# The recurrence's three kinds of column sums share the accumulator banks of its scores, and the filler's matmuls rotate over three banks in place of two

## The chip, the cores and the metric

The kernel runs on one core of one Trainium2 chip. The metric is the device time of one execution in microseconds (us). The kernel before took 2701.37 us, the median of three runs that lay between 2699.15 and 2703.07 us. The names of the engines are those of the profile: PE multiplies matrices (PEld is its loading of the stationary matrix, which lies beside the multiplications), DVE is the vector engine, ACT the scalar engine, POOL the engine of small auxiliary work, SP the engine that issues most transfers (DMA).

## The reference, cut to what matters

The program is a decoder trunk of two layers over 1024 positions of width 1024, in float32. Each layer adds a mixer and then a gated feed-forward network (FFN) to the residual. The mixer of layer 0 is attention beside a pooling mixer; the mixer of layer 1 is a linear recurrence (RWKV-7) over 16 heads of 64 columns. The change touches the recurrence of layer 1 and the FFN work that runs beside it.

```python
kk = heads(k * k_k.astype(f32))
kk = kk / jnp.maximum(jnp.sqrt(jnp.sum(kk * kk, axis=-1, keepdims=True)), 1e-12)
...
def _rwkv7_step(state, inp):
    r_t, w_t, k_t, v_t, a_t, b_t = inp
    sa = jnp.einsum('bhvk,bhk->bhv', state, a_t)
    state = (state * w_t[:, :, None, :] + sa[..., None] * b_t[:, :, None, :]
             + v_t[..., None] * k_t[:, :, None, :])
    return state, jnp.einsum('bhvk,bhk->bhv', state, r_t)
...
mean = jnp.mean(y, axis=-1, keepdims=True)
var = jnp.mean(jnp.square(y - mean), axis=-1, keepdims=True)
y = ((y - mean) * lax.rsqrt(var + GN_EPS)).reshape(b, s, d) * ln_w.astype(f32) + ln_b.astype(f32)
bonus = jnp.sum(rh * kh * r_k.astype(f32), axis=-1, keepdims=True) * vh
...
def _swiglu(h, w_gate, w_up, w_down):
    return (jax.nn.silu(h @ w_gate) * (h @ w_up)) @ w_down
```

## The kernel before

Activations lie transposed: 128 channels on the partitions, 512 positions (one half of the sequence) along the free axis. So every large accumulator is 128x512 float32, which is one whole PSUM bank, and a core has eight banks. A large product is made in three matmuls, because each operand is split into a rounded high part and a low remainder: weight high by activation high (L163), weight high by activation low (L164), weight low by activation high (L165). For that each weight block is loaded by DMA into `wraw`, ACT casts it to `whi` (L151) and DVE makes `wlo` (L152). An output block of a projection takes 24 matmuls (8 blocks of the inner dimension by 3); a block of the FFN's down projection takes 12, since the 22 blocks of the FFN's hidden width are taken in groups of four.

**The recurrence.** One half of the sequence and eight heads make a job (`Rwkv.job`); there are four, in the order (heads 0 to 7, half 0), (heads 8 to 15, half 0), and later the same two for half 1. By the trace they begin at about 1050, 1284, 1776 and 2000 us. A job works in chunks of 64 positions and has three stages.

1. Preparation, for four pairs of heads one after the other. A pair loads decay, key, a, r and v, squares the key and sums the squares over each head's 64 channels by a matmul with a block matrix (L1025, result `ms`); ACT turns the sum into a reciprocal root (L1028, L1029) and DVE builds the operands `ZL` and `bk` with it (L1030, L1032, L1038, L1040). Then come the scores: four accumulators (two batches of chunks by two heads, L1056), which ACT and DVE evict into `XR` and `ZL` (L1061 to L1064). Small products with the identity and a centring matrix follow (L1070, L1081).
2. Inversion of the triangular blocks, on DVE: a transpose (L1092, L1095), 30 steps of two small operations (L1106, L1108), then the transposes back, into `t11` (L1116) and into `XR` (`back`, L1114). Two further rounds on PE finish it: `gps` (L1126) needs `t11`, its result is copied to `g` half by ACT (L121) and half by DVE (L123), and `xps` (L1136) needs both halves of `g`.
3. The serial loop over eight chunks (L1161, L1167, L1173, L1184, L1186), with the bonus of one pair beside every second chunk (`head_sum`, L970), then the group norm's sum of squares (L1201) and the four gated outputs (L1212, L1217 to L1219).

**The filler.** The work beside a job is FFN work: in half 0 the second half's FFN of layer 0 (`f1`), in half 1 the output projection and the first half's FFN of layer 1 (`rest`). `weave` takes a step of the job and then as many filler matmuls as the numbers in `rw.fr` say. A filler block takes an accumulator from `k.mm`, here the tag `fm` of the pool `pf`. A gate block is read for the last time by DVE at L726, after three ACT operations (L723 to L725); an up block at L732; a down block by the residual add at L705.

**Banks and order.** A pool tile is asked for by tag and number of buffers, and the tags rotate: the n-th tile with the tag `s` of three buffers lies in the bank of the (n-3)-rd, and its first matmul waits until that one's last reader is done. During the jobs the eight banks were: tag `t` one (the three kinds of sums), tag `s` three (scores and the loop's first two products), tag `o` two, tag `fm` two. The order on each engine is fixed when the program is built, by a scheduler that reorders the recorded instructions; an engine runs its list strictly in order, so a matmul that waits for a bank holds back everything behind it on PE.

## Time and profile before

| what | value |
|---|---|
| median of the runs | 2701.37 us (2699.15 to 2703.07) |
| time of the profiled execution | 2699.03 us |
| its span from first to last instruction | 2697.2 us |
| PE busy | 2633.8 us (98%), 15368 matmuls |
| PEld busy | 2080.5 us (77%) |
| DVE busy | 1724.3 us (64%) |
| ACT busy | 1301.9 us (48%) |
| mean granted TensorE clock | 0.993 |

A busy time is the share in which an engine had an instruction under way; the rest is split by what ended the idle time. The chain of waits follows the work that ended last back from the last instruction. In rows of the trace the first two figures are the start and the duration in us; a bracket at the end gives the idle time of the engine just before the instruction, and who ended it. The granted clock of a stretch is 1.00 where PE runs at 2.4 GHz throughout; the other level is 1.2 GHz.

### The profile page before, as it was taken

The numbers are of one execution on the slowest core, as the hardware profiler recorded it, in microseconds if no ns is written. First come the engines' busy times: TensorE is split into PE (matmuls) and PEld (weight loads), VectorE is DVE, ScalarE is ACT, GpSimd is POOL, SyncE is SP. The second block draws the span as 40 slices with busy tenths as digits, with TensorE's granted clock in tenths as the row PEclk, the third lists the DMA queues.
The fourth block names the chain that finished last, engine by engine and source line by source line (L and its number), as shares of the span: only waits on it lengthen the run. The fifth ranks groups of instructions, "written<-read, shape, count | busy, mean of one in ns | idle before, by whom it ended". The sixth has DMA issues, their size and how long they took to land.

```text
span 2697.2 us, 40269 instructions
## 1 busy us (share of the span) xinstructions
PE 2633.8 (98%) x15368; PEld 2080.5 (77%) x15368; DVE 1724.3 (64%) x2940; ACT 1301.9 (48%) x2299; POOL 50.6 (2%) x139
## 2 busy tenths in 40 slices
PE   8999999999999999999999999999999999999999
PEld 6787878788888777777777677777777778888887
DVE  8777684654446655975995685469768856634443
ACT  7555564442224765534634466664445444332232
POOL 1000000000001000000000000000000000000000
PEclk9999999999999999999999999999999999999999
DMA  4111131233333546424523534454344336333333
GB/s 136 58 52 55 44 98 48 83 97 96 96 98 114 168 162 191 129 82 123 160 87 100 194 101 161 160 182 128 91 141 134 93 100 199 109 98 94 98 98 94
DMA packets 170817, 307.03 MB, mean 114 GB/s; under 512 B 18928, under 2 KB 25968, under 8 KB 170624
## 3 DMA queue, kind: packets, MB, share of 16 engines
q1 hardware_dynamic: 156800, 279.29, 33.6%
q10 hardware_dynamic: 13824, 25.17, 2.5%
q8 instruction: 120, 1.97, 0.3%
q14 instruction: 73, 0.60, 0.1%
HBM read 257.96 MB, written 46.43 MB: 113 GB/s over the span
## 4 chain that ended last, share of the span: by engine, by line
PE 77%; DVE 14%; DMA 3%; ACT 3%; issue 2%; SPq 0%; DVEq 0%; ACTq 0%
PE mm L163 16%; PE mm L164 16%; PE mm L165 16%; PE fm L163 6%; PE fm L164 5%; PE fm L165 5%; DVE wlo L152 2%; PE mm L175 1%; DVE nu L1108 1%; DVE pd L1106 1%; DMA wraw<-in_wu_dram 1%; DVE ZL L1064 1%; ACT whi L151 1%; PE o L1173 1%; PE s L1161 1%
## 5 line engine op out<-in xcount | busy, mean ns | idle before, releaser
L151 ACT CAST whi<-wraw 128x512 fp32r<-128x512 f32 x738 | 453.7, 617 | 867.4 <-PE mm L164 478.7
L152 DVE TENSOR_TENSOR wlo<-wraw,whi 128x512 fp32r<-128x512 f32 x738 | 501.3, 684 | 449.6 <-ACT whi L151 441.1
L163 PE MATMUL mm<-hh,whi 128*128 128x512 f32 x864 | 344.1, 400 | 6.2 <-ACT hh L355 6.1
L165 PE MATMUL mm<-hh,wlo 128*128 128x512 f32 x864 | 338.4, 392 | 0.0
L164 PE MATMUL mm<-hl,whi 128*128 128x512 f32 x864 | 337.9, 392 | 0.0
L163 PE MATMUL mm<-uh,whi 128*128 128x512 f32 x728 | 283.6, 391 | 0.9 <-DVE x L1317 0.9
L165 PE MATMUL mm<-uh,wlo 128*128 128x512 f32 x728 | 283.1, 390 | 1.0 <-DVE wlo L152 1.0
L164 PE MATMUL mm<-ul,whi 128*128 128x512 f32 x728 | 283.2, 390 | 0.0
L163 PE MATMUL fm<-h1h,whi 128*128 128x512 f32 x528 | 220.2, 417 | 14.8 <-DVE sg L726 9.9
L164 PE MATMUL fm<-h1l,whi 128*128 128x512 f32 x528 | 210.3, 398 | 0.1
L165 PE MATMUL fm<-h1h,wlo 128*128 128x512 f32 x528 | 209.5, 397 | 0.5 <-DVE wlo L152 0.5
L163 PEld LDWEIGHTS mm<-hh,whi 128*128 128x128 f32 x864 | 162.3, 188 | 43.4 <-ACT hh L355 7.8
L165 PEld LDWEIGHTS mm<-hh,wlo 128*128 128x128 f32 x864 | 162.5, 188 | 34.4 <-issue 0.2
L164 PEld LDWEIGHTS mm<-hl,whi 128*128 128x128 f32 x864 | 162.7, 188 | 33.1 <-DVE hl L260 1.7
L163 PE MATMUL fm<-hh,whi 128*128 128x512 f32 x416 | 170.9, 411 | 3.3 <-ACT hh L259 2.3
L164 PE MATMUL fm<-hl,whi 128*128 128x512 f32 x416 | 164.9, 396 | 0.2 <-DVE hl L260 0.2
L165 PE MATMUL fm<-hh,wlo 128*128 128x512 f32 x416 | 164.6, 396 | 0.0
L163 PEld LDWEIGHTS mm<-uh,whi 128*128 128x128 f32 x728 | 136.5, 188 | 34.6 <-issue 3.5
L164 PEld LDWEIGHTS mm<-ul,whi 128*128 128x128 f32 x728 | 136.6, 188 | 30.9 <-issue 1.1
L165 PEld LDWEIGHTS mm<-uh,wlo 128*128 128x128 f32 x728 | 136.7, 188 | 30.1 <-DVE wlo L152 1.8
L705 DVE TENSOR_TENSOR x<-mm,x 128x512 f32<-128x512 f32 x96 | 66.3, 692 | 119.3 <-PE mm L165 119.2
L163 PEld LDWEIGHTS fm<-h1h,whi 128*128 128x128 f32 x528 | 100.6, 191 | 47.1 <-DVE sg L726 12.2
(338 smaller groups left out, 4645.4 us busy)
## 6 DMA issues: line engine op xcount, KB each, us to landing
wraw<-in_wg_dram SPq DMA_DIRECT2D x176, 256.0 KB, 2.8
wraw<-in_wu_dram SPq DMA_DIRECT2D x176, 256.0 KB, 2.7
wraw<-in_wd_dram SPq DMA_DIRECT2D x176, 256.0 KB, 2.7
wraw<-in_w_in_dram SPq DMA_DIRECT2D x52, 256.0 KB, 2.9
x<-in_xT_dram SPq DMA_DIRECT2D x32, 256.0 KB, 4.6
x<-x SPq DMA_DIRECT2D x32, 256.0 KB, 3.3
wraw<-in_w_k_dram SPq DMA_DIRECT2D x32, 256.0 KB, 2.8
wraw<-in_w_v_dram SPq DMA_DIRECT2D x32, 256.0 KB, 3.0
```

What stands on the lines that cost most here:

```text
L151: k.nc.scalar.copy(hi[0:p, 0:n], raw[0:p, 0:n])
L152: k.nc.vector.tensor_tensor(lo[0:p, 0:n], raw[0:p, 0:n], rd(hi[0:p, 0:n]), ALU.subtract)
L163: nc.tensor.matmul(out, wh, xh, start=(first and i == 0), stop=False)
L164: nc.tensor.matmul(out, wh, xl, start=False, stop=False)
L165: nc.tensor.matmul(out, wl, xh, start=False, stop=(last and i == n - 1))
L175: k.nc.tensor.matmul(out[n * q:n * q + n], w[:, n * j:n * j + n], xs[j], start=c == 0, stop=c + g == len(xs), tile_position=(0, n * q))
L705: nc.vector.tensor_tensor(X[half][m], o, X[half][m], ALU.add)
L1064: nc.vector.tensor_tensor(ZL[h][HS[1 - h], i, bs], s4[HS[1]], self.msk[HS[1]].rearrange("p a t -> p (a t)").unsqueeze(1).broadcast_to([64, ...
L1106: nc.vector.tensor_tensor(pv, nu[:, j + 1:32, j:j + 1].broadcast_to([P, n, j]), nu[:, j:j + 1, 0:j].broadcast_to([P, n, j]), ALU.mult)
L1108: nc.vector.tensor_tensor(nu[:, j + 1:32, 0:j], nu[:, j + 1:32, 0:j], pv, ALU.add)
L1161: nc.tensor.matmul(z[HS[h], i], ZL[h][:, i, c, 0:64], SV[h][:, i, c], start=True, stop=True)
L1173: nc.tensor.matmul(sp[HS[h], i], BK[h][:, i, c], uv[h][:, i], start=True, stop=True)
```

## The change

Three accumulators of the recurrence no longer have a bank with the tag `t` of their own: the sum of squares of the key (L1022 asks for it, L1025 writes it), the bonus sum in `head_sum` (L968, L970) and the group norm's sum of squares (L1197, L1201). They ask for the tag `s` with `k.sbufs` buffers, which is three in both recurrence stages, and so take turns with the scores and with the loop's products. The bank that the tag `t` had goes to the filler: the tag `fm` gets three buffers in place of two, in the three places where the filler's accumulators are set. The count of banks stays at eight. Layer 0's attention keeps its tag `t`.

```diff
     def head_sum(self, src):
 
         k = self.k
-        o = pst(k, "t", 1)
+        o = pst(k, "s", k.sbufs)
...
             nc.scalar.activation(kn, kr, AF.Square, scale=cvec(k, "k_k", p))
-            ms = pst(k, "t", 1)
+            ms = pst(k, "s", k.sbufs)
...
         nc.scalar.copy(spread, raw)
-        z = pst(k, "t", 1)
+        z = pst(k, "s", k.sbufs)
...
-    f1 = using(k, f1, mm=(pf, "fm", 2), ntbufs=3)
+    f1 = using(k, f1, mm=(pf, "fm", 3), ntbufs=3)
...
-    k.mm, k.sigm, rw.ln_exp = (pf, "fm", 2), False, True
+    k.mm, k.sigm, rw.ln_exp = (pf, "fm", 3), False, True
...
-    project, rest = (using(k, g, mm=(pf, "fm", 2), ntbufs=3) for g in tail(0, tp, 4, False))
+    project, rest = (using(k, g, mm=(pf, "fm", 3), ntbufs=3) for g in tail(0, tp, 4, False))
```

No instruction is added or removed, but the scheduler sets some in another order.

**Place 1: PE, the first job, the sum `ms` of its second pair.** `t_9657` and `s_9657` are the same sum; `fm_9605` and `fm_9718` are filler blocks, `s_9495`, `s_9541` and `s_9542` scores of the first pair, `o_9620` its centred v. Before:

```order
L165 MATMUL fm_9605<-h1h_5371,wlo_9600 128x512
L1025 MATMUL t_9657<-kn_9655,cc 128x512
L163 MATMUL fm_9605<-h1h_5377,whi_9599 128x512
L164 MATMUL fm_9605<-h1l_5378,whi_9599 128x512
L165 MATMUL fm_9605<-h1h_5377,wlo_9600 128x512
L163 MATMUL fm_9718<-h1h_5335,whi_9706 128x512
L164 MATMUL fm_9718<-h1l_5336,whi_9706 128x512
L165 MATMUL fm_9718<-h1h_5335,wlo_9707 128x512
L1056 MATMUL s_9495<-ZL_2218_9414,bk_9483 128x128
```

Now:

```order
L164 MATMUL fm_9718<-h1l_5348,whi_9706 128x512
L1056 MATMUL s_9542<-ZL_2219_9415,bk_9483 128x128 x4
L1081 MATMUL o_9620<-cc,ld_9491 64x64 x16
L1025 MATMUL s_9657<-kn_9655,cc 128x512
L165 MATMUL fm_9718<-h1h_5347,wlo_9707 128x512
```

The sum stood ahead of the first pair's scores and now stands behind the last of them, 11 filler matmuls later; the second pair's scores come 17 filler matmuls later than they did. By the products at L1081 of the third pair the count of filler matmuls that stand ahead is the same as before. The fourth pair moves likewise (its sum by 30, its scores by 20 filler matmuls), and from its products at L1081 to the end of the job PE's list is the same. Over the four jobs, 6 of the 12 sums that follow another pair moved by 7 filler matmuls or more, the others by 0 or 1.

**Place 2: DVE, the end of the first job's inversion.** `sg_10570` belongs to the filler blocks `fm_10530` (gate) and `fm_10587` (up), `t_2457_10609` is `t11`, `g_10679` is DVE's half of `g`. Before:

```order
L1116 STREAM_TRANSPOSE t_2457_10609<-nu_10216 128x32x32
L1114 STREAM_TRANSPOSE XR_9416<-nu_10216 32x32x32 x2
L152 TENSOR_TENSOR wlo_10634<-wraw_10635,whi_10633 128x512
L152 TENSOR_TENSOR wlo_10741<-wraw_10742,whi_10740 128x512
L1114 STREAM_TRANSPOSE XR_9416<-nu_10216 32x32x32
L726 TENSOR_TENSOR sg_10570<-fm_10530,sg_10570 128x512
L1114 STREAM_TRANSPOSE XR_9416<-nu_10216 32x32x32
L152 TENSOR_TENSOR wlo_10797<-wraw_10798,whi_10796 128x512
L732 TENSOR_TENSOR sg_10570<-fm_10587,sg_10570 128x512
L152 TENSOR_TENSOR wlo_10817<-wraw_10818,whi_10816 128x512
L260 TENSOR_TENSOR h1l_10624<-sg_10570,h1h_10623 128x512
L123 COPY g_10679<-s_10646 32x512
```

Now:

```order
L1116 STREAM_TRANSPOSE t_2457_10609<-nu_10216 128x32x32
L1114 STREAM_TRANSPOSE XR_9416<-nu_10216 32x32x32 x2
L726 TENSOR_TENSOR sg_10570<-fm_10530,sg_10570 128x512
L152 TENSOR_TENSOR wlo_10741<-wraw_10742,whi_10740 128x512
L152 TENSOR_TENSOR wlo_10797<-wraw_10798,whi_10796 128x512
L1114 STREAM_TRANSPOSE XR_9416<-nu_10216 32x32x32
L732 TENSOR_TENSOR sg_10570<-fm_10587,sg_10570 128x512
L1114 STREAM_TRANSPOSE XR_9416<-nu_10216 32x32x32
L260 TENSOR_TENSOR h1l_10624<-sg_10570,h1h_10623 128x512
L123 COPY g_10679<-s_10646 32x512
L152 TENSOR_TENSOR wlo_10817<-wraw_10818,whi_10816 128x512
```

The last read of the gate block moved ahead of two weight remainders and a transpose; `wlo_10634` moved ahead of L1116 and `wlo_10817` behind the copy of `g`, so that one remainder less stands ahead of that copy.

**Place 3: DVE, the end of the second job.** `gn` are the four gated outputs, `x_4130` to `x_4467` the residual adds that free the down blocks `fm_14189`, `fm_14245`, `fm_14323` and `fm_14343`, in this order on PE. Before:

```order
L1218 SCALAR_TENSOR_TENSOR gn_14217<-gn_14217,cv,ld_14213 128x512
L1217 SCALAR_TENSOR_TENSOR gn_14232<-BK_2681_11850,cv,o_14226 128x512
L1219 TENSOR_TENSOR gn_14217<-gn_14217,ld_14215 128x512
L1218 SCALAR_TENSOR_TENSOR gn_14232<-gn_14232,cv,ld_14228 128x512
L705 TENSOR_TENSOR x_4130<-fm_14189,x_4130 128x512
L1219 TENSOR_TENSOR gn_14232<-gn_14232,ld_14230 128x512
L705 TENSOR_TENSOR x_4260<-fm_14245,x_4260 128x512
L152 TENSOR_TENSOR wlo_14378<-wraw_14379,whi_14377 128x512
L152 TENSOR_TENSOR wlo_14398<-wraw_14399,whi_14397 128x512
L705 TENSOR_TENSOR x_4367<-fm_14323,x_4367 128x512
L152 TENSOR_TENSOR wlo_14404<-wraw_14405,whi_14403 128x512
L705 TENSOR_TENSOR x_4467<-fm_14343,x_4467 128x512
```

Now:

```order
L1219 TENSOR_TENSOR gn_14202<-gn_14202,ld_14200 128x512
L1217 SCALAR_TENSOR_TENSOR gn_14217<-BK_2681_11850,cv,o_14211 128x512
L1217 SCALAR_TENSOR_TENSOR gn_14232<-BK_2681_11850,cv,o_14226 128x512
L1218 SCALAR_TENSOR_TENSOR gn_14217<-gn_14217,cv,ld_14213 128x512
L1218 SCALAR_TENSOR_TENSOR gn_14232<-gn_14232,cv,ld_14228 128x512
L1219 TENSOR_TENSOR gn_14217<-gn_14217,ld_14215 128x512
L1219 TENSOR_TENSOR gn_14232<-gn_14232,ld_14230 128x512
L705 TENSOR_TENSOR x_4130<-fm_14189,x_4130 128x512
L705 TENSOR_TENSOR x_4260<-fm_14245,x_4260 128x512
L705 TENSOR_TENSOR x_4367<-fm_14323,x_4367 128x512
L152 TENSOR_TENSOR wlo_14358<-wraw_14359,whi_14357 128x512
L152 TENSOR_TENSOR wlo_14378<-wraw_14379,whi_14377 128x512
```

All twelve operations on `gn` now stand ahead of the residual adds, and `wlo_14358`, which stood among them, stands behind the adds.

## Rows read from the trace of the kernel before

**Rows 1.** The page's busy times.

```profile
PE 2633.8 (98%) x15368; PEld 2080.5 (77%) x15368; DVE 1724.3 (64%) x2940; ACT 1301.9 (48%) x2299; POOL 50.6 (2%) x139
```

**Rows 2.** What PE waited for over the whole span: the waiting line, the releaser, the total in us, the number of waits, the longest.

```profile
PE fm L163 <- DVE sg L726: 13.2, 8, 4.0
...
PE fm L163 <- DVE x L705: 5.9, 6, 3.0
PE s L1056 <- DVE ZL L1064: 5.5, 6, 1.9
...
PE s L1126 <- DVE t L1116: 4.1, 2, 2.3
```

**Rows 3.** Busy time by stretch: start and end, length, then busy us (and instructions) of PE, PEld, DVE, ACT and POOL, the granted clock, the busy share of the DMA engines and GB/s. The stretches are preparation and inversion of the first job, the same of the second, and the inversion of the fourth up to PE's wait for `t11`.

```profile
1054.00:1118.00 64.00, 60.07 (x441) 45.94 (x441) 61.66 (x99) 37.73 (x71) 3.76 (x7) 0.97 0.48 150
1118.00:1161.50 43.50, 42.06 (x211) 33.88 (x210) 41.59 (x90) 21.14 (x38) 0.75 (x6) 1.00 0.34 104
...
1284.00:1352.00 68.00, 63.77 (x477) 48.63 (x478) 63.80 (x100) 40.98 (x74) 3.02 (x7) 0.97 0.48 145
1352.00:1391.00 39.00, 34.62 (x161) 27.95 (x158) 37.09 (x85) 17.33 (x31) 0.76 (x6) 0.97 0.35 102
...
2080.00:2125.00 45.00, 41.75 (x276) 33.41 (x276) 43.18 (x93) 19.94 (x35) 1.62 (x7) 1.00 0.29 89
```

**Rows 4.** The five longest of PE's waits for a filler bank, from its timeline.

```profile
1169.21 0.50 PE L163 MATMUL fm<-h1h,whi 128*128 128x512 f32 x1 [4.03 <-DVE sg L726]
...
1366.66 0.50 PE L163 MATMUL fm<-h1h,whi 128*128 128x512 f32 x1 [1.67 <-DVE sg L726]
1388.76 0.79 PE L163 MATMUL fm<-h1h,whi 128*128 128x512 f32 x1 [2.71 <-DVE sg L726]
...
1508.27 0.76 PE L163 MATMUL fm<-h1h,whi 128*128 128x512 f32 x1 [3.00 <-DVE x L705]
...
2050.06 0.50 PE L163 MATMUL fm<-gh,whi 128*128 128x512 f32 x1 [2.35 <-DVE sg L726]
```

**Rows 5.** Stretches around these five waits, columns as in rows 3.

```profile
1164.00:1178.00 14.00, 9.97 (x89) 7.50 (x88) 11.10 (x12) 3.05 (x5) 0.00 (x0) 0.76 0.28 78
1386.00:1396.00 10.00, 7.29 (x26) 5.88 (x26) 9.66 (x19) 2.35 (x5) 0.00 (x0) 0.83 0.22 62
1507.00:1513.00 6.00, 4.74 (x14) 3.84 (x15) 3.64 (x7) 0.35 (x1) 0.00 (x0) 0.72 0.55 177
2049.00:2055.00 6.00, 4.94 (x15) 3.90 (x16) 4.34 (x7) 3.88 (x7) 0.00 (x0) 0.72 0.39 122
...
1364.00:1372.00 8.00, 6.33 (x28) 4.91 (x27) 7.72 (x19) 3.53 (x6) 0.00 (x0) 1.00 0.38 108
```

**Rows 6.** The end of the first job's inversion: the timeline of DVE, and of PE from 1174 us on.

```profile
1173.92 0.70 DVE L123 COPY g<-s 32x512 f32<-32x512 f32 x1
...
1174.85 0.63 PE L164 MATMUL fm<-h1l,whi 128*128 128x512 f32 x1
...
1178.00 0.39 PE L164 MATMUL fm<-h1l,whi 128*128 128x512 f32 x1
...
1178.55 1.20 PE L1136 MATMUL s<-XR,g 32*32 32x32 f32 x64
```

**Rows 7.** The same place in the second job: DVE's copy of `g`, and PE.

```profile
1406.26 0.70 DVE L123 COPY g<-s 32x512 f32<-32x512 f32 x1
...
1407.31 1.20 PE L1136 MATMUL s<-XR,g 32*32 32x32 f32 x64
```

**Rows 8.** The end of the second job, from the timelines of DVE and of PE.

```profile
1498.94 0.69 DVE L705 TENSOR_TENSOR x<-fm,x 128x512 f32<-128x512 f32 x1
...
1507.43 0.69 DVE L705 TENSOR_TENSOR x<-fm,x 128x512 f32<-128x512 f32 x1
...
1504.87 0.40 PE L165 MATMUL fm<-h1h,wlo 128*128 128x512 f32 x1
```

**Rows 9.** The waits for `t11` in the third and fourth job, and the DVE operations that set when the fourth job's third batch of scores could start, with its start on PE.

```profile
1896.19 1.20 PE L1126 MATMUL s<-t,XR 32*32 32x32 f32 x64 [1.82 <-DVE t L1116]
...
2124.03 1.20 PE L1126 MATMUL s<-t,XR 32*32 32x32 f32 x64 [2.25 <-DVE t L1116]
...
2054.70 0.69 DVE L705 TENSOR_TENSOR x<-fm,x 128x512 f32<-128x512 f32 x1 [1.30 <-PE fm L165]
2055.31 0.68 DVE L1040 TENSOR_TENSOR bk<-ld,ld 128x512 f32<-128x512 f32 x1
...
2056.45 2.05 PE L1056 MATMUL s<-ZL,bk 64*128 64x128 f32 x24
```

**Rows 10.** The operations between a sum `ms` and the scores of its pair, of the first job, by line: count, busy us, mean ns of one, idle time before.

```profile
L1028 ACT ACTIVATE kn<-t,eps 128x512 f32<-128x512 f32 x6 | 4.1, 682 | 0.4 <-PE t L1025 0.4
L1029 ACT ACTIVATE kn<-kn 128x512 f32<-128x512 f32 x6 | 3.8, 630 | 0.1
...
L1032 DVE SCALAR_TENSOR_TENSOR ZL<-kn,cv,ep 64x512 f32<-64x512 f32 x11 | 8.2, 744 | 0.1
L1030 DVE SCALAR_TENSOR_TENSOR kn<-kn,ld 128x512 f32<-128x512 f32 x6 | 4.1, 685 | 0.0
L1038 DVE SCALAR_TENSOR_TENSOR ld<-kn,vc,ld 128x512 f32<-128x512 f32 x5 | 3.7, 750 | 0.1
L1040 DVE TENSOR_TENSOR bk<-ld,ld 128x512 f32<-128x512 f32 x5 | 3.4, 685 | 0.0
```

## The prediction

> **What bounds the kernel now.** I read the busy times first [rows 1]: PE is busy in 2633.8 of 2697.2 us, so all its idle time together is 63.4 us, and that is the most that any change of waits can give, but for the clock. The list of PE's waits comes next [rows 2]. The reader is to see that two of its entries are waits for a filler bank: L163 opens a filler block and can do so only when the block two before it has been read by L726 (13.2 us in 8 waits) or by L705 (5.9 us in 6), together 19.1 us. Their places [rows 4] are the inversions of the first two jobs, the end of the second job and the preparation of the fourth.
>
> Third comes the granted clock around these waits [rows 5]. After the wait of 4.03 us it averages 0.76 over 14 us, which is 14 x 0.24 = 3.4 us of full-speed work lost; after 2.71, 3.00 and 2.35 us it loses 10 x 0.17, 6 x 0.28 and 6 x 0.28, 1.7 us each time; around the wait of 1.67 us the clock stays at 1.00. A filler matmul's row reads 0.63 us in the slow stretch and 0.39 us behind it [rows 6]. So the four longest waits cost 8.5 us more than they show, and the whole account of the filler's banks is 19.1 + 8.5 = 27.6 us.
>
> Last I asked which engine was behind in these stretches [rows 3]. In preparation and inversion of the first job DVE was busy 61.66 of 64.00 and 41.59 of 43.50 us, idle 4.25 us in 107.5; in the second 63.80 of 68.00 and 37.09 of 39.00, idle 6.1 us in 107. PE idled 5.4 and 8.6 us in the same stretches, more than DVE. PE waited there because DVE was late with everything, the filler's reads among the rest. That decides most of the sum.
>
> **The change part by part.** No instruction comes or goes, so what counts is waits, order and clock.
>
> *The third bank, end of the second job.* PE stopped at 1505.27 us (1504.87 + 0.40) [rows 8] until L705 of `x_4130` had ended at 1508.1, and that add stood behind the output operations. With three banks the block that waited takes the bank of `fm_14150`, which L705 had freed at 1499.6. It runs from 1505.3 to about 1508.0 (12 matmuls by 0.23 us, from 28 in 6.33 us in the last of rows 5). The block behind it needs the bank of `fm_14189`. In the new order the twelve output operations stand ahead of that bank's add (place 3), but they are the same twelve that stood among what ran up to 1508, and one weight remainder less stands among them, so I expect the add near 1508 and no new wait. DVE is not saturated behind this place, and PE is the bound up to the norm. So the whole 3.00 us goes and the slow stretch with it: -4.7 us. The bounds are -4.7 and 0 (if the next block waits for its `wlo`, which now stands behind the adds).
>
> *The third bank, first job.* The waits there add up to 5.5 us (three of L726; the longest 4.03). But the step behind them, L1136, needs DVE's half of `g`. That copy ended at 1174.62 and L1136 began at 1178.55 [rows 6]; in the second job it began 0.35 us after the copy (1406.96 and 1407.31) [rows 7]. The slack is 3.93 - 0.35 = 3.6 us. One weight remainder less stands ahead of the copy (place 2), 0.6 to 0.7 us. So L1136 can come 4.2 us earlier, no more unless DVE idles less. The 4.03 us of idle time moves from L163 to L1126 and L1136, and a slow stretch follows it there, in work that PE alone bounds: 1.7 to 3.4 us given back. Net -0.8 to -2.5, and up to 2 us more if half of DVE's idle time goes. I take -2; bounds -5 and +1.
>
> *The third bank, second job.* The waits are 1.67 + 2.71 + 0.6 (two of L705) us, but L1136 began 0.35 us after the copy of `g`, so there is no slack at all. DVE could win back part of its 6.1 us; against that the slow stretch of 1.7 us that lay ahead of L1136, where PE had time, now lies behind it. I take 0; bounds -4 and +3.
>
> *The third bank, third and fourth job.* There L1126 itself waited 1.82 and 2.25 us for DVE's `t11` [rows 9]: a PE that comes sooner waits longer. In the fourth job the wait of 2.35 us at 2050 us is followed by scores that began at 2056.45, 0.5 us after DVE's last operand was ready (2055.31 + 0.68); DVE had idled 1.30 us there for the late filler block, and that goes. But PE then waits for the scores, with a slow stretch to follow. I take -0.5 for both jobs; bounds -4 and +2.
>
> *The sums in the ring of the scores.* This cost the trace of before doesn't show. `ms` of a pair must now wait until the third tile before it, the second of the four score tiles of the pair ahead, has been evicted, so it stands behind these scores (place 1). Behind `ms` come L1028, L1029, L1030, twice L1032, L1038 and L1040: 0.68 + 0.63 + 0.69 + 1.49 + 0.75 + 0.69 = 4.9 us until the pair's scores may start [rows 10]. Before, this ran beside the eviction of the pair ahead. It is hidden if DVE and PE have other work meanwhile. On PE they have: the scores of the first job's second pair come 17 filler matmuls, 17 x 0.23 = 3.9 us, later, and the lists agree again a pair later. On DVE the order puts `bk`, `ZL` and weight remainders of later steps there. From below it costs 0; from above the full 4.9 us for each pair but the first of the four jobs, 12 x 4.9 = 59 us, which is far out of reach, since only 6 of the 12 sums moved on PE by more than one filler matmul. I keep 0 and 8 us (half of 4.9 at three or four places) as ends and take +1, near the lower one, because the moved pair has work on both engines. The bonus sums and the norm's sum stand in the serial loop, where DVE has idle time and each tile is read before its bank comes round: 0, with the serial chain as the cover; if it were gone, one eviction of 0.7 us for each of 16 sums, 11 us.
>
> The sum is -4.7 - 2 + 0 - 0.5 + 1 = -6.2 us. Against the profiled execution's own 2699.03 us (span 2697.2, 1.8 us around it) that is 2692.8. The profiled execution was 2.3 us below the median of the runs, so for a median I add 2.3: 2695.1, rounded to 2695 us.
>
> The Trainium skill has a rule that would make more of it and one that would make less. "Perfetto Trace Analysis", section Identifying Performance Opportunities, says that gaps which repeat on the engine that should be saturated can mean too little PSUM for the next tile; the waits for filler banks are such gaps, and by that rule the whole account of rows 2 would go, the first rival below. The same page, Identifying the Most-Contended Engine, says to take occupancy for VectorE as a fair measure and to improve the busiest engine first; DVE's 96% in rows 3 bears that out for the inversions, and by it the banks give next to nothing there, the second rival.
>
> **The rivals.**
>
> - *The whole account goes.* All 19.1 us and the slow stretches' 8.5: 2701.4 - 27.6 = 2674; with half of it, 2688. For it: the waits are for banks, and the PE order is kept. Against it: DVE's idle time of 4.25 and 6.1 us.
> - *Given back.* PE's idle time only changes its name, from L163 to L1126, L1136 and L1056, also at the end of the second job, because of the `wlo` behind the adds. 2697 to 2703, the centre 2700. For it: rows 3 and 9. Against it: rows 8, where DVE had room soon after.
> - *Slower by the ring.* The sums bind the pairs of a job together: DVE idles while PE and ACT pass the 4.9 us from `ms` to the scores, so each inversion starts later, and since it ends in L1126 and L1136, for which PE already waits in two jobs, that delay is PE's. At 2 us for each of six moved sums it is +12, with the -4.7 of the end of job two +7: 2708. It decides from about 2 us of delay per moved sum. For it: DVE is the late engine in these stretches. Against it: the order gives DVE other operations meanwhile.
> - *The third bank is never reached*, because the scheduler put each block's read early anyway: then the waits at L163 stay, and the time is 2700. It can hardly be: in the built order the matmul that waited at 1508 us no longer waits for DVE.
>
> **How the numbers follow.** This kernel's measurement can tell about 0.2%, 5.4 us, from no change; so faster means below 2696. The forecast case, a gain of 3 to 12 us, has 0.49, of which 0.34 lies below 2696 and 0.15 above. The whole account or most of it (a gain over 12) has 0.16. Given back, with the bank never reached, has 0.21. Slower by the ring has 0.14. That makes faster 0.50, no change 0.36, slower 0.14. The likeliest case alone spans 2689 to 2699. The range of 8 in 10 goes from 2682 (some 70% of the whole account) to 2705 (the ring's lower prices).
>
> **What the profile would show.** The list of PE's waits has lost L163 for L726 and for L705 (under 3 us together). If I am right, L1126 and L1136 have gained several us for DVE, above all L1136 for the copy of `g` in the first two jobs; the wait at the end of the second job is gone, and the clock stays at 1.00 there; DVE's idle time in rows 3's stretches is about what it was. If the first rival is right, L1126 and L1136 wait no more than before and DVE idles less. If the ring costs, L1056 or L1025 wait longer, for L1064 or L1040, and DVE idles more ahead of L1030. I am wrong in size if PE's total idle time of 63.4 us falls by more than 15 us or grows, and wrong in the mechanism if the gain lies in the inversions of the first two jobs.

## The result and the profile after

The changed kernel takes 2711.36 us (median of 7 runs, 2705.91 to 2714.29) against 2699.96 us for the kernel before on the same chip (7 runs). The ratio is 1.0039, interval 1.0028 to 1.005, which is 10.5 us of 2700 (7.6 to 13.5). It is slower; the forecast was 2695 us, and the range ended at 2705. Medians below leave out two executions that took several times as long as the others, one of all_but_ms (6304.43 us) and one of early_ring_of_four (10087.19 us).

The profiled execution spans 2709.6 us. The page's busy times, which answer to [rows 1]:

```profile
PE 2634.0 (97%) x15368; PEld 2088.6 (77%) x15368; DVE 1725.0 (64%) x2940; ACT 1301.8 (48%) x2299; POOL 50.5 (2%) x139
```

PE does the same 2634 us of work. Its idle time went from 63.4 to 2709.6 - 2634.0 = 75.6 us, 12.2 of the 12.4 us between the spans. (That says where the time stands, not what caused it: the mean granted clock fell as well, from 0.993 to 0.988.) So the list of PE's waits is read next, with the columns of [rows 2]:

```profile
PE s L1056 <- DVE bk L1040: 15.0, 13, 3.8
PE s L1056 <- DVE ZL L1064: 8.8, 10, 1.7
PE s L1126 <- DVE t L1116: 7.5, 3, 3.7
...
PE s L1136 <- ACT g L121: 5.2, 1, 5.2
PE s L1136 <- DVE g L123: 3.4, 2, 2.1
...
PE mm L163 <- ACT hh L259: 2.9, 1, 2.9
...
PE fm L163 <- DVE x L705: 1.2, 2, 0.6
PE fm L163 <- DVE sg L726: 1.2, 1, 1.2
```

The reader is to see two things. The third bank did what it says: L163 waits 2.4 us for L705 and L726, where it waited 19.1 [rows 2]. But other entries have grown or are new: the scores (L1056) for `bk`, from 4.3 us in the listing by line of the kernel before to 15.0; the scores for L1064, the eviction of scores ahead, from 5.5 to 8.8; L1126 from 4.1 to 7.5; L1136, which is not in the list of the kernel before; and L163 of the layer's first product for `hh`, 2.9 us.

Where on the way is the time lost? A mark that comes once in each job is the first product of the serial loop, L1161. From the timeline of PE of the kernel before:

```profile
1193.49 0.69 PE L1161 MATMUL s<-SV,ZL 128*64 128x64 f32 x16
...
1422.25 0.69 PE L1161 MATMUL s<-SV,ZL 128*64 128x64 f32 x16
...
1917.49 0.69 PE L1161 MATMUL s<-SV,ZL 128*64 128x64 f32 x16
...
2146.37 0.69 PE L1161 MATMUL s<-SV,ZL 128*64 128x64 f32 x16
```

and of the changed kernel:

```profile
1195.08 0.69 PE L1161 MATMUL s<-SV,ZL 128*64 128x64 f32 x16
...
1427.83 0.69 PE L1161 MATMUL s<-SV,ZL 128*64 128x64 f32 x16
...
1927.06 0.69 PE L1161 MATMUL s<-SV,ZL 128*64 128x64 f32 x16
...
2154.02 0.69 PE L1161 MATMUL s<-SV,ZL 128*64 128x64 f32 x16
```

The delay is 1.6, 5.6, 9.6 and 7.7 us at the four marks, and 12.4 us at the end. So the second and third job lose 4 us each, the fourth wins 2 back, and nearly 5 us come behind the last job, in a place of which the prediction does not speak.

A mark comes from a single execution, and the runs show how much that leaves open. Four pairs of them run the same instructions in the same order on PE, DVE and ACT until 2290 us, since they differ only in where the last norm stands: the kernel before and norm_early_before, the changed kernel and tail_cover, and two pairs further below (the runs are told in the next section). Their marks differ by 0.2 to 1.7 us in 14 of 16 cases, and by 2.0 and 3.7 us in two. tail_cover has its marks at 1193.36, 1428.55, 1928.12 and 2154.20 us, so the large delays of the second and third job are there again, but the 1.6 us of the first job are not.

**The second job.** PE, ACT and DVE between the sum `ms` of its second pair and that pair's scores, from the timelines of the changed kernel (an idle time before an instruction and its releaser stand in brackets):

```profile
1298.03 1.02 PE L1025 MATMUL s<-kn,cc 128*128 128x512 f32 x2
...
1298.30 0.63 ACT L1008 ACTIVATE ep<-ld 128x512 f32<-128x512 f32 x1
1298.96 0.63 ACT L1016 ACTIVATE ld<-ld 128x512 f32<-128x512 f32 x1
1299.49 0.67 ACT L1028 ACTIVATE kn<-s,eps 128x512 f32<-128x512 f32 x1
...
1301.64 0.69 DVE L1030 SCALAR_TENSOR_TENSOR kn<-kn,ld 128x512 f32<-128x512 f32 x1
...
1305.12 0.68 DVE L705 TENSOR_TENSOR x<-fm,x 128x512 f32<-128x512 f32 x1
1305.72 0.68 DVE L1040 TENSOR_TENSOR bk<-ld,ld 128x512 f32<-128x512 f32 x1
...
1306.45 1.46 PE L1056 MATMUL s<-ZL,bk 64*128 64x128 f32 x16 [3.76 <-DVE bk L1040]
```

In the timeline of the kernel before, the second sum of this job ran at 1287.29 us, 16.8 us ahead of its scores:

```profile
1287.29 1.13 PE L1025 MATMUL t<-kn,cc 128*128 128x512 f32 x2 [0.35 <-ACT kn L1021]
...
1304.07 2.01 PE L1056 MATMUL s<-ZL,bk 64*128 64x128 f32 x22
```

Now it runs at 1298.03, behind all 32 scores of the pair ahead. From there the scores are not 4.9 but 8.4 us away: 1.0 us is the sum itself, which the 4.9 leave out, and on ACT the sum finds L1008 and L1016 ahead of it, on DVE other operations, an add of the filler (L705) among them. The filler on PE lasts until 1302.69, 4.7 us from the start of the sum, and then PE stands 3.76 us.

So the path was not made longer by the change; what went is the lead. In the kernel before, 7 of the 16 sums ran 12.5 to 18.7 us ahead of their pair's first scores, and the other 9 ran 7.4 to 9.3 us ahead. In the changed kernel all 16 run 7.2 to 9.2 us ahead.

**Behind the last job.** The last norm of the first half's outputs, from PE's timeline of the kernel before, with the last filler matmul behind it and the layer's first matmul:

```profile
2322.53 1.02 PE L307 MATMUL mm<-sq,cc 128*128 128x512 f32 x2
...
2333.76 0.39 PE L165 MATMUL fm<-gh,wlo 128*128 128x512 f32 x1
2333.99 0.39 PE L163 MATMUL mm<-hh,whi 128*128 128x512 f32 x1
```

and of the changed kernel:

```profile
2340.42 0.40 PE L165 MATMUL fm<-gh,wlo 128*128 128x512 f32 x1
2340.66 1.02 PE L307 MATMUL mm<-sq,cc 128*128 128x512 f32 x2
2344.55 1.44 PE L163 MATMUL mm<-hh,whi 128*128 128x512 f32 x3 [2.87 <-ACT hh L259]
```

Before, the filler's last blocks stood behind the norm, and PE worked through them while the norm was turned into `hh`. With three banks they all stand ahead of the norm, none is left behind it, and PE waits 2.87 us. The granted clock around such places, with the columns of [rows 3]; the stretches are the end of the first job's inversion, the third job's second scores, the wait of 3.76 us, the norm, and the place where the wait of 3.00 us at the end of the second job [rows 4] has shrunk to 0.57 us:

```profile
1173.00:1185.00 12.00, 8.52 (x85) 6.72 (x87) 7.01 (x9) 5.51 (x10) 0.00 (x0) 0.57 0.25 74
1793.00:1808.00 15.00, 10.09 (x84) 9.30 (x85) 14.34 (x23) 9.23 (x18) 0.83 (x2) 0.58 0.41 127
1306.00:1312.00 6.00, 5.55 (x37) 4.36 (x38) 5.46 (x9) 2.11 (x6) 0.20 (x1) 0.72 0.72 205
2343.00:2349.00 6.00, 4.45 (x13) 3.50 (x14) 5.86 (x9) 2.54 (x5) 0.00 (x0) 0.72 0.02 6
1513.00:1519.00 6.00, 5.43 (x25) 4.21 (x24) 4.08 (x7) 0.60 (x1) 0.00 (x0) 1.00 0.59 205
```

At the norm it is 2.87 us of idle time and 6 x 0.28 = 1.7 us of work at half clock, together 4.6 us, against the 4.7 us by which the delay grows behind the last mark.

### The profile page after: what moved, and what is told of

Read it like the earlier page. It is cut to its first block, busy times and chain, and to the rows that moved or that the text cites. A ratio compares the mean times of both kernels' runs of the same rounds, so it can differ in the third digit from the quotient of the medians.

```text
span 2709.6 us, 40268 instructions
## 1 busy us (share of the span) xinstructions
PE 2634.0 (97%) x15368; PEld 2088.6 (77%) x15368; DVE 1725.0 (64%) x2940; ACT 1301.8 (48%) x2299; POOL 50.5 (2%) x139
## 4 chain that ended last, share of the span: by engine, by line
PE 76%; DVE 14%; ACT 4%; DMA 3%; issue 3%; SPq 0%; DVEq 0%; ACTq 0%; POOL 0%
PE mm L163 16%; PE mm L164 16%; PE mm L165 16%; PE fm L163 6%; PE fm L165 5%; PE fm L164 5%; DVE wlo L152 2%; DVE pd L1106 1%; DVE nu L1108 1%; PE mm L175 1%; DMA wraw<-in_wd_dram 1%; ACT whi L151 1%; DMA wraw<-in_wu_dram 1%; PE o L1173 1%; PE s L1161 1%
## 5 line engine op out<-in xcount | busy, mean ns | idle before, releaser
L163 PE MATMUL mm<-hh,whi 128*128 128x512 f32 x864 | 344.4, 401 | 9.5 <-ACT hh L355 6.3
L163 PE MATMUL mm<-uh,whi 128*128 128x512 f32 x728 | 283.6, 391 | 0.9 <-DVE x L1317 0.9
L163 PE MATMUL fm<-h1h,whi 128*128 128x512 f32 x528 | 219.3, 416 | 5.2 <-DVE sg L732 1.6
L163 PEld LDWEIGHTS mm<-hh,whi 128*128 128x128 f32 x864 | 162.6, 189 | 47.2 <-ACT hh L355 7.4
L163 PE MATMUL fm<-hh,whi 128*128 128x512 f32 x416 | 172.1, 414 | 2.3 <-ACT hh L259 2.3
L163 PEld LDWEIGHTS mm<-uh,whi 128*128 128x128 f32 x728 | 136.5, 188 | 34.6 <-issue 3.5
L705 DVE TENSOR_TENSOR x<-mm,x 128x512 f32<-128x512 f32 x96 | 66.2, 691 | 120.1 <-PE mm L165 120.0
L163 PEld LDWEIGHTS fm<-h1h,whi 128*128 128x128 f32 x528 | 100.7, 191 | 34.7 <-issue 8.4
```

Source lines behind the costliest of these rows:

```text
L163: nc.tensor.matmul(out, wh, xh, start=(first and i == 0), stop=False)
L705: nc.vector.tensor_tensor(X[half][m], o, X[half][m], ALU.add)
```

## The experiments

Two theories stood at the start. A: the sums in the ring of the scores cost the time, since each pair's `ms` waits behind the scores of the pair before. B: the third bank itself costs it, since filler that runs ahead is missing as cover later. Ratios below are against runs of the kernel before on the same chip, and a ratio is turned into us by 2700.

**ring_alone** is the kernel before with only the three sums moved (the same edit at `o`, `ms` and `z`); the freed bank lies unused:

```diff
-            ms = pst(k, "t", 1)
+            ms = pst(k, "s", k.sbufs)
```

> The three sums share the scores' three banks, the filler keeps two, one bank stays unused. Theory A (the shared ring costs: a pair's sum now waits behind the scores of the pair ahead, and the 4.9 us from the sum to the next scores lie open): 2706 to 2710 us, PE's wait of L1056 for L1040 near the 15 us of the changed kernel (4.3 before), the first product of the serial loop late by 1 to 5 us in the first three jobs; the waits of L163 for L726 and L705 stay near 19 us, and no wait of 2.9 us for the norm's output at 2344 us. Theory B (the third filler bank costs, by letting the filler run ahead and use up what covered later waits): 2700 us within 3, L1056 for L1040 near 4.3 us.

Measured: 2707.16 us, ratio 1.0024 (1.0013 to 1.0035), +6.5 us. PE's waits in it:

```profile
PE s L1056 <- DVE bk L1040: 10.5, 9, 3.4
PE s L1056 <- DVE ZL L1064: 9.6, 10, 2.1
PE fm L163 <- DVE sg L726: 9.6, 7, 2.6
PE fm L163 <- DVE x L705: 8.3, 6, 3.0
PE s L1126 <- DVE t L1116: 4.1, 2, 2.3
```

The wait for `bk` is there without the third bank, and L1126 has not grown and L1136 waits 0.5 us in this listing. The wait for L1064 has grown too, from 5.5 [rows 2] to 9.6 us. (The profiled execution was the fastest of the seven, 2703.05 us, so its waits may be smaller than usual.) So more than half of the loss is the ring's, and the growth of L1126 and L1136 comes with the third bank.

**bank_from_scores** asks for B alone: the sums stay in the transposes' bank, the filler has three banks, and the scores pay with one of theirs:

```diff
-    k.sbufs = 3
+    k.sbufs = 2
...
-    k.mm, k.sigm, rw.ln_exp = (pf, "fm", 2), False, True
+    k.mm, k.sigm, rw.ln_exp = (pf, "fm", 3), False, True
```

> The sums keep their own bank, the filler has three, and the scores give up one: two in place of three. Theory A: the sums stand as before; with the loss of 4.6 us at the end of the kernel that goes with three filler banks, and whatever two score banks cost, 2700 to 2708 us; L1056 waits longer for L1064 (the evictions) but not for L1040. Theory B: 2709 to 2716 us, with L1126 and L1136 waiting as in the changed kernel (16 us in all against 4 before).

Measured: 2712.45 us, ratio 1.0056 (1.0043 to 1.0068). (The same edit of `fm` stands in all three places.) A's forecast is missed in the time and in the wait for L1040, but the run doesn't decide for B either: the scores' ring is smaller too, and L1056 waits 8.6 us for `bk`, so that two effects are mixed. What it does show beside ring_alone is that a third filler bank brings L1126 to 8.2 us and L1136 to 5.9 for ACT, wherever the bank comes from.

**tail_cover** is the changed kernel with one line more, by which the norm of the first half's outputs is recorded ahead of the filler's last blocks:

```diff
     weave(project, (fill, TS))
+    next(rest)
     run(fill)
```

> The changed kernel with one line more: the norm ahead of the last feed-forward network is recorded before the filler's last blocks, so that these can stand behind it on PE. Both theories: the wait of 2.87 us at 2344 us and the half clock of 3.4 us behind it go, 4.6 us, so 2706 to 2707 us if they were what the end of the kernel lost. Rival (the wait only moves to the next place, or the order of other work changes as much): 2710 to 2713 us.

Measured: 2707.13 us (2703.83 to 2712.38), ratio 1.0033 (1.002 to 1.0046). The wait for `hh` fell from 2.9 to 0.5 us. The median is 4.2 us lower, as expected; the ratio is lower by 0.0006 only, less than its interval, so this run alone settles no size.

**norm_early_before** is its control: the same line on the kernel before.

> The kernel before with the norm of the first half's outputs recorded ahead of the filler's last blocks, a control for the 4.2 us that this gave on the changed kernel. In the kernel before 45 filler matmuls stand behind the last norm already, so if those 4.2 us were the cover that the third bank used up, it gives nothing here: 2699 to 2703. If the earlier norm is good whatever stands behind it (rival): 2696 to 2698.

Measured: 2700.92 us, ratio 0.9996 (0.9988 to 1.0004): nothing, as expected. So it is not the earlier norm by itself that helps; early_and_tail below shows it again where the filler behind the norm has been used up.

**ms_early** is the changed kernel in which the next pair's load, square, sum and the two activations behind it are recorded ahead of the scores of the current pair:

```diff
+        def key(i, p):
...
+            ms = pst(k, "s", k.sbufs)
...
+            nc.tensor.matmul(ms, bones, kn, start=True, stop=True)
...
+            if i < 3:
+                nxt = yield from key(i + 1, pr[i + 1])
```

> The changed kernel, but each pair's sum of squares, with its logarithm and exponential on ScalarE, is recorded ahead of the scores of the pair before it, so that in the shared ring it no longer waits for their eviction; banks as in the changed kernel. Theory A: the jobs lose what they lost (1.4, 4.0 and 4.8 us in the first three) and the gain of the third bank shows: 2699 to 2704 us, L1056 for L1040 back under 7 us. Theory B: 2709 to 2713 us, as the changed kernel, since the banks are the same.

Measured: 2700.44 us, ratio 1.0007 (0.9998 to 1.0016): 8.6 us of the 10.5 have come back, and L1056's wait for `bk` is gone from the list. Theory B's forecast of 2709 to 2713 us is out by far.

**early_old_banks** is the control for that order: the sums early, but in the transposes' bank, and the filler with two.

> The kernel before with one edit: the next pair's sums recorded ahead of the current pair's scores; the three sums stay in the transposes' bank, the filler keeps two banks. A control for the earlier order of the sums: if it only takes back what the scores' ring costs (A), it gives nothing here, 2698 to 2702, since the kernel before has no wait of L1056 for L1040 over 1 us in its list. If the earlier order is good by itself, whatever the ring (rival), 2688 to 2694, and then the gain of 11 us against the changed kernel says little of the ring.

Measured: 2699.14 us, ratio 0.9993 (0.9984 to 1.0002), -1.9 us. The kernel before does have waits of L1056 for L1040, 4.3 us in all with a longest of 1.2, and they are gone here. The earlier order gives at most 4 us by itself; the rest of the 8.6 us is the ring's price taken back.

**only_ms** and **all_but_ms** divide the three sums: in the first `ms` alone is moved, in the second the head sums and the norm's sum.

> The kernel before with one of the three sums in the scores' ring, the sum ahead of each pair's scores (ms); the two others in the transposes' bank, the filler with two banks. A: this one carries the ring's cost: 2705 to 2708, as with all three (2707.2), and L1056 waits 8 to 12 us for L1040. Rival (the bonus sums, two matmuls each on the chain from the scores to the outputs, cost as much or more): 2700 to 2703.

> The other half: the head sums and the norm's sum in the scores' ring, ms in the transposes' bank, the filler with two banks. A: 2699 to 2702, L1056 waits under 2 us for L1040. Rival (the cost lies with any sum that takes a place in the ring): 2703 to 2706, half or more of the 7.2 us of all three.

Measured: only_ms 2707.18 us, ratio 1.002 (1.0011 to 1.0029), all_but_ms 2700.08 us, ratio 0.9998 (0.9987 to 1.0008). The expectation of under 2 us for the wait for `bk` in all_but_ms was careless: the kernel before has 4.3 itself, and all_but_ms 3.9. With only_ms it is 11.7. `ms` carries the ring's cost, and the other two sums cost nothing that can be told from noise (some 2 us at most).

**ring_of_four** is ring_alone with the freed bank given to the scores' tag, so the three sums stand in a ring of four.

```diff
-    k.sbufs = 3
+    k.sbufs = 4
```

> The kernel before with the three sums in the scores' tag and the freed bank given to that tag: four banks in the ring, the filler with two. If the sums cost because they take places from the scores (the ring is too small), the fourth place takes most of it back: 2700 to 2703, L1056 waits 4 to 6 us for L1040. If they cost by their turn (a sum asks for its bank behind the 32 scores of the pair before it, in a ring of three or of four; A), little comes back: 2705 to 2708, L1056 waits 9 us or more for L1040.

Measured: 2700.92 us, ratio 0.9995 (0.9987 to 1.0003). Each side was half right. The wait for `bk` did not fall, it rose, in the listing by line (count, busy us, mean ns of one, idle time before and its releasers) from

```profile
L1056 PE MATMUL s<-ZL,bk 64*128 64x128 f32 x512 | 54.1, 291 | 11.0 <-DVE ZL L1064 5.5 <-DVE bk L1040 4.3 <-DVE ZL L1045 1.1
```

in the kernel before to

```profile
L1056 PE MATMUL s<-ZL,bk 64*128 64x128 f32 x512 | 36.7, 299 | 18.5 <-DVE bk L1040 18.5
```

but the time came back, as the rival said. So the total of this wait is not the price. How much work DVE gets done while a job is prepared comes nearer to it. The stretch of the third job's preparation by columns of [rows 3], of the kernel before:

```profile
1776.00:1850.00 74.00, 69.45 (x468) 54.16 (x467) 65.67 (x105) 49.90 (x91) 3.27 (x9) 0.98 0.55 177
```

of ring_of_four:

```profile
1776.00:1850.00 74.00, 62.44 (x431) 48.87 (x430) 61.86 (x97) 47.08 (x85) 2.94 (x9) 0.91 0.51 161
```

and of ms_early:

```profile
1776.00:1850.00 74.00, 69.53 (x477) 52.62 (x476) 67.71 (x109) 48.74 (x91) 5.54 (x11) 0.98 0.54 173
```

The third number with brackets is DVE. Beside the start of the third and fourth job's first L1161 (in the early kernels it is line 1168), each from its kernel's one profiled execution:

| kernel | sum `ms` | DVE busy, 1776 to 1850 | third job's mark | fourth job's mark |
|---|---|---|---|---|
| before | own bank | 65.67 | 1917.5 | 2146.4 |
| all_but_ms | own bank | 63.02 | 1920.5 | 2150.1 |
| ring_of_four | late, four places | 61.86 | 1923.1 | 2149.1 |
| ring_alone | late, three places | 61.47 | 1922.5 | 2150.8 |
| only_ms | late, three places | 60.20 | 1924.0 | 2152.2 |
| the changed kernel | late, three places, third bank | 58.67 | 1927.1 | 2154.0 |
| ms_early | early, three places, third bank | 67.71 | 1915.7 | 2142.4 |

With one exception (ring_of_four and ring_alone), the less work DVE has done by 1850 us, the later the serial loop begins: 3.8 us less and 5.6 us later in ring_of_four, 2.0 more and 1.8 earlier with the sums early. Part of this is carried in from the jobs ahead. By the job's first scan on DVE (L1005), only_ms enters it 3.4 us later than the kernel before, the changed kernel 4.9, ring_alone 1.5, the others of this table within 0.8. From that scan to the mark the third job takes 136.1 us in the kernel before, 134.5 in ms_early, 138.3 in all_but_ms, and 139.2 to 141.4 in the four kernels with the late sum: by this measure the late sum costs the job 3 to 5 us. bank_from_scores, where the sum keeps its bank, takes 139.0 as well, so a longer job can have other causes.

ring_of_four pays in the third job like the rest; by the marks it is 1.7 and 1.2 us ahead of the kernel before in the first two jobs (1191.77 and 1421.06) and makes up half of its delay in the fourth. Its profiled execution ends 2.9 us after that of the kernel before while its median lies 0.8 us lower, so the marks don't show where all of the price came back.

**early_ring_of_four** was to tell whether the late sum still costs in the ring of four, hidden by a gain beside it:

> The freed bank given to the scores' tag (a ring of four), the filler with two, and the next pair's sums recorded ahead of the current pair's scores. In the ring of four with the late sums, L1056 waited 18.5 us for L1040, yet the time came back to 2700.9: either the late turn of the sums still costs there and something of like size was gained beside it (the 32 scores of a pair run in one piece, L1056 busy 36.7 us for 54.1), or the turn costs nothing once the ring has four places. If it still costs (A), the earlier order takes the wait for L1040 under 2 us and gives 5 to 9 us here: 2692 to 2696. If four places are what the sums lacked (rival), the earlier order gives nothing more: 2699 to 2702.

Measured: 2699.76 us, ratio 0.9995 (0.9986 to 1.0004): by the time, the rival's case. By the marks the early order does give its 7.6 us in the third job (1915.53 for 1923.10), and they are lost again by the fourth (2149.14 for 2149.08). So the late sum costs in a ring of four as well, at one job, and the kernel doesn't keep what its removal gives. Why the fourth job takes it back was not tried by itself, but the next runs show a part of it.

**early_two_banks** takes the third bank out of ms_early (filler with two, one bank unused), and **early_and_tail** joins the two remedies on the changed kernel, with all its banks.

> The kernel with the sums in the ring and recorded early (2700.4 us with three filler banks), with two filler banks in their place; one bank lies unused. It tells what the third bank itself is worth. If its waits only move to other instructions of the jobs and it costs the 4.2 us at the norm (B), this is 2695 to 2698. If the third bank saves in the jobs what it costs at the norm, 2699 to 2702; if it saves more, above 2702.

> The changed kernel with both findings undone: the sums of the next pair are recorded ahead of the current pair's scores, and the norm of the first half's outputs ahead of the filler's last blocks. If the two losses are separate (each a piece of TensorE's line without work behind it, at another place), they add: 2711.4 - 11 (the sums) - 4.2 (the norm) = about 2696, range 2693 to 2699, below the kernel before; L1056's waits for L1040 at 0 and the wait for hh L259 under 1 us. If what is saved at one place is only waited for at the next (the rival: VectorE's work bounds the jobs whatever stands on TensorE), it stays at 2699 to 2702.

Measured: early_two_banks 2698.57 us, ratio 0.9986 (0.9976 to 0.9996); early_and_tail 2694.6 us (12 runs, 2688.91 to 2701.47), ratio 0.9978 (0.9969 to 0.9987), -5.9 us: faster than both kernels, and the fastest here. early_two_banks lies between its two forecasts. It differs from ms_early by the third bank alone, so with the sums early the third bank costs 0.0021, 5.7 us (2 to 9 by the two intervals), while its loss at the norm stands. The earlier norm takes 0.0029, 7.8 us (4 to 11), off; the row's 4.6 us is what the trace accounts for. The marks show where the third bank earns something: with it the fourth job's mark comes at 2142.42 (ms_early) and 2142.61 (early_and_tail), without it at 2147.47 (early_two_banks) and 2149.14 (early_ring_of_four). (early_old_banks has it at 2146.94, early_tail_old_banks below at 2145.73.) So what the early sums win in the third job is kept in the fourth only with three filler banks. The wait that goes with it is that for the filler's banks. Between its third and fourth mark early_two_banks has

```profile
PE fm L163 <- DVE sg L726: 5.8, 4, 1.8
```

and ms_early has no wait of L163 there at all. From mark to mark this is 232.4 against 226.8 us. All of PE's waits in that stretch come to 10.3 and 8.0 us, since some move to other lines with the third bank; the rest of the difference stands in PE's busy time.

PE's waits over the whole of early_and_tail, where the edit moves the lines by seven (L1133 is L1126, L1143 is L1136):

```profile
PE s L1143 <- ACT g L121: 5.8, 2, 5.1
PE s L1133 <- DVE t L1123: 5.6, 2, 3.6
...
PE s L1143 <- DVE g L123: 3.4, 3, 2.4
```

The waits for `bk` are gone, but L1126's and L1136's have stayed: most of the waits for filler banks have turned into these.

**early_tail_old_banks** keeps both earlier orders and puts the banks back as they were.

> The fastest kernel so far (2694.6 us) with the banks of the kernel before: both earlier orders stay, the sums go back to the transposes' bank and the filler to two. If the moved banks are worth something once the orders pay for them, this is slower than 2694.6: 2698 to 2701, as with the earlier order of the sums alone (2699.1). If the two orders by themselves make the gain (rival), it is 2693 to 2696.

Measured: 2699.28 us, ratio 0.9987 (0.9978 to 0.9996). It is 4.7 us above early_and_tail by the medians and 2.4 us (0.0009) by the ratios, with intervals that overlap, and the two runs were made on different chips. So it looks as if the moved banks were worth some 2 to 5 us once both orders pay for them, but that is not shown.

## Why the prediction was wrong

**What bounds the kernel** was read rightly in one half. That PE's waits for filler banks in the inversions would only change their name, because DVE is late there, is what the trace shows: 16.7 us of them went, and L1126 and L1136 have 12.0 us more between them. The Trainium skill, "Perfetto Trace Analysis", section Identifying Performance Opportunities, says that repeated gaps on the engine that should be saturated can mean too little PSUM. The trace agrees that these gaps were of that kind, since a bank more closed 16.7 of their 19.1 us, but the time did not go with them, as the first rival had it. The half that was wrong is the bound of what a change of waits can do: idle time can also be added. The prediction's own sign of being wrong in size, that PE's idle time grows, came true.

**The sums in the ring** is the first of two steps that failed: "I keep 0 and 8 us ... as ends and take +1, near the lower one, because the moved pair has work on both engines". It measured +6.5 us (interval 3.5 to 9.5). The mechanism was in the prediction, as the third rival, with its price of about +7 net and the rows that would show it (L1056 for L1040). And it looked for DVE's idle time ahead of L1030, which grew (the third job: 3.7 us in 3 waits for 0.9 in one). What was wrong is the cover. I took the 17 filler matmuls that stand between as enough against 4.9 us, but the path from `ms` to the scores took 8.4 us at 1298.03. One us of that is the sum itself, which the 4.9 leave out (its rows [rows 10] take in six sums, the first job's and two of the second's), and some 2.5 us are operations that were to cover the path on ACT and DVE and stand in line ahead of it. The rows of the kernel before could have told that: no sum there was followed by its scores in less than 7.4 us. The operations in that line cover a wait on PE and lengthen the chain that passes through DVE at the same time. "It is hidden if DVE and PE have other work meanwhile" was therefore the wrong test where DVE is 94% busy [rows 3]. The other sums were put at 0, and the time of all_but_ms bears that out. ms_early shows the step from the other side: with the lead given back and the ring as it was, 8.6 of the 10.5 us are gone.

**The third bank** is the second. Its four terms came to -7.2 us; what it adds to ring_alone is 10.5 - 6.5 = +4.0 us (0 to 8 by the two intervals). The next three parts say where that lies.

**The end of the second job**, the largest term, -4.7 us, had its place right: the wait of 3.00 us is 0.57 now and the clock there 1.00. But I asked what is late next only up to the next block. PE came to a later block sooner than its inputs, and stood there, as the changed kernel's timeline shows:

```profile
1541.84 0.47 PE L163 MATMUL fm<-h1h,whi 128*128 128x512 f32 x1 [1.61 <-DVE sg L732]
1543.09 1.22 PE L163 MATMUL fm<-h1h,whi 128*128 128x512 f32 x2 [0.77 <-ACT h1h L259]
```

Thirty us on, 2.4 us of the gain are given back, and the clock averages 0.79 over the 8 us from 1540 us (1.00 in the kernel before), another 1.7 us of work. From the second job's L1161 to the norm behind that job, the delay falls only from 5.6 us to 4.2 (L307 at 1552.59 before, at 1556.75 after): -1.4 and not -4.7. (tail_cover has -1.7 there, 6.3 to 4.6.)

**The first two jobs and the last two**, -2, 0 and -0.5 us. The place that the prediction named, L1136 at the end of the first job's inversion [rows 6], reads in the changed kernel's timeline:

```profile
1175.15 0.31 PE L1136 MATMUL s<-XR,g 32*32 32x32 f32 x2 [5.21 <-ACT g L121]
1176.79 1.91 PE L1136 MATMUL s<-XR,g 32*32 32x32 f32 x62 [1.33 <-DVE g L123]
```

The step comes 1.8 us earlier than 1178.55, not 4.2, and the 1.91 us for 62 matmuls go with a slow clock: 0.57 over 12 us, 5.2 us of work, where 1.7 to 3.4 were allowed. The wait of 4.03 us at L163 became one of 6.5 us here. The reason lies ahead of this place. DVE begins the transposes back 3.6 us later than it did, in the timeline of the kernel before

```profile
1159.24 2.22 DVE L1116 STREAM_TRANSPOSE t<-nu 128x1024 f32<-128x1024 f32 x1
```

and of the changed kernel

```profile
1162.88 2.19 DVE L1116 STREAM_TRANSPOSE t<-nu 128x1024 f32<-128x1024 f32 x1
```

ring_alone has the same delay (1163.28) and is not late at its first mark (1193.36): the slack of 3.6 us ahead of L1136, which the prediction gave to the third bank, takes it up. So ring and third bank draw on the same slack. With the sums early DVE begins at 1159.39, and in the timeline of ms_early the step (L1143 there) comes 4.3 us earlier than before, as the term had it:

```profile
1174.21 1.91 PE L1143 MATMUL s<-XR,g 32*32 32x32 f32 x62 [0.54 <-DVE g L123]
```

The place and the size of that step were right by themselves, then, and failed with the ring. What is left of them at the job's mark, 0.7 and 1.7 us in early_and_tail and ms_early against early_two_banks, is within what marks differ by. What the third bank earns in the fourth job is 3 to 7 us by the marks once the sums come early; the prediction had -0.5 there, with -4 as its end.

**Behind the last job** the prediction has no term. It looked at the order of the jobs, not at what uses up the filler: a third bank lets the scheduler place filler earlier everywhere, and the last stretch that filler covered, the norm, lay open. That is 4.6 us by the rows, and tail_cover, early_and_tail and norm_early_before show that it is this cover and not the norm's order by itself.

Put together, as rough sizes: the ring is 5.5 us above its term, and the third bank 11.2 us above its terms (+4.0 for -7.2); together these are the 16.7 us between the forecast change of -6.2 and the measured +10.5. Of the 11.2 us, the norm has 4.6 and the end of the second job 3.3. The 3.3 us that are left belong to the four jobs, where the ring, as the first job shows, takes up slack that the third bank was to use; the runs don't divide them further, since the ratios have intervals of 2 to 3 us to each side.

## What to carry to other kernels

A tile that joins another tag's ring inherits the program order of that ring: before sharing, look at which tile stands as many allocations earlier as the ring has buffers, and record the newcomer ahead of the long batch (here a place more in the ring did it too). Cover for a chain has to be read on every engine that the chain passes through, not only on the one that waits. When a buffer more lets filler run ahead, ask where the filler ends, since the last place that it covered is the one that opens. And a wait that disappears can't be priced until the next wait on the same engine has been found.

## What was not expected

The idle time of the saturated engine did not rank the kernels. ring_of_four has PE busy 2619.2 of 2700.1 us, 80.9 us of idle time and 17.5 more than the kernel before, with a wait of 18.5 us on one line, and takes the same time: its scores run 32 in one piece (L1056 is busy 36.7 us for 54.1 before), and the page's busy time of PE fell by 14.6 us. So busy time can count the gaps between matmuls that are spread out as work.

How dear a wait is did not follow from its length. Behind the wait of 3.76 us at 1306.45 us the clock averages 0.72 over 6 us, which is 1.7 us of work. Around a shorter one, in the third job, it averages 0.58 over 15 us, near its lower level of 1.2 GHz, which is 6.3 us; more waits of PE follow it there, so not all of that is its own. From the changed kernel's timeline:

```profile
1796.28 3.35 PE L1056 MATMUL s<-ZL,bk 64*128 64x128 f32 x22 [3.35 <-DVE bk L1040]
```

One thing stays open: with the sums early and two filler banks, the third job wins and the fourth gives it back. The waits for the filler's banks are a part of that; no run was made for the rest.
